# Splitting weights in pieces of 1024 columns from a ring of three, with other rates for the late modulation

## The chip, the cores and the metric

One Trainium2 chip, one core of it. The metric is the device time of one execution in microseconds (us). TensorE runs the matrix products (PE in the profile, its weight loads PEld), VectorE (DVE) and ScalarE (ACT) the elementwise work, GpSimd (POOL) a few small powers, and SyncE (SP) starts nearly all DMA transfers. Each engine works through its own instructions in the order in which they stand; semaphores order the engines among each other.

## The reference

One layer of a diffusion backbone over 256 latent tokens and 256 context tokens, width 2048, in fp32:

```python
h = modulate(rmsnorm(x, norm_mix), sh1, sc1) @ w_in        # and the same for ctx
y_mla = attention(q, k, v)                  # 8 heads, low rank q and kv, latents see all keys
o_dn  = gated_delta_net(q, k, v, g, beta)   # 8 heads, chunks of 64, a scan in each direction
merged = sigmoid(ga) * (y_mla @ w_o_mla) + sigmoid(gb) * (dn_output(o_dn) @ w_o_dn)
x = x + g1 * (merged @ w_out)
gate, val = split(modulate(rmsnorm(x, norm_ffn), sh2, sc2) @ w_ffn_up, 2)
x = x + g2 * ((silu(dwconv(gate)) * val) @ w_ffn_down)
```

The six modulation vectors sh1, sc1, g1, sh2, sc2, g2 are `silu(c) @ w_ada + b_ada`. The hidden width of the feed-forward is 5504.

## The kernel before

Every activation lies transposed in SBUF, features on the 128 partitions and 256 tokens along the free axis. Products with weights are made in two parts: a weight tile `raw` is loaded by DMA, ACT rounds it to `whi` (the fp32r type), and DVE takes `wlo = raw - whi`. Activations are kept in the same way as a pair of 256 columns, high and low. `mm_hl` then makes two matmuls for each 128 rows of depth: `whi` against both parts (512 columns) and `wlo` against the high part (256 columns). On PE these pairs are nearly all of the work.

`load_w` loads a weight row in pieces of up to `GR` = 1024 columns, from a ring of `NR` = 5 places `raw`, and splits each piece in chunks of `GH` = 512 columns from a ring of `NH` = 6 places for `whi` and six for `wlo`. A place comes free for the next load or split when its last reader is done. 1024 columns are eight pairs of matmuls. `lazy_w` calls `load_w` piece by piece as they are needed. The first stage of the kernel (norm, first modulation, first projections, 864 columns each) has its own tiles and does not use the ring.

The stages, in order: the first stage; the heads of the delta net (with their projections, `mmp`); the attention (with products for gates, `gtp`, put in between as filler); the scan of the delta net (with gate products and branch products, `brp`, as filler); the branch products of the delta net; the output projection (`ops`, 16 tiles, each followed by `gather`, which adds the two halves of the product with ACT and DVE into `yx`, then `x1`, its square on ACT, and the sum of squares `ssq` on DVE); the second norm (`ss` a sum over partitions, `ms`, a power on POOL, the broadcast `bc_ps`); the feed-forward (`fps`, 43 tiles each of gate and value); the down projection (`dps`, 16 tiles of depth 43).

`h2_tile(k)` makes one 128-row slice of the normed, modulated input of the feed-forward: `h` on DVE, `h` on ACT, then its high and low parts `H`. The first four feed-forward products (gate and value of tiles 0 and 1) run together over the slices while these are made, in four quarters of 512 columns of the weights.

The late modulation (the vectors g1, sh2, sc2, g2) is work for DVE: 128 tiles `rawa` of 128 x 1024 from `w_ada`, each multiplied with a row of silu(c) (`sch`) and summed in one instruction, followed by one that reads the sum (`parts`). The tiles go through the same ring `raw` and SP's queue as the weights. `ada_rest` is a generator; between its tiles it yields a price, and `Side` runs it as far as the time credited to it allows. `sch` is loaded anew at each change of the half of silu(c), with some yields ahead of the load and behind it. The credits: in the heads `ADB / 22600` of the filler's time, in the attention `AD`, in the scan `ADS` of the step's price, 1500 for each tile of the output projection, 1000 for each of the feed-forward. Three of the four vectors have to be ready before the feed-forward, so what is owed then is run at once:

```python
    while ada.done < 3:
        ada(1)
```

A scheduler places the instructions of each engine; on PE in the first stage and in the heads, the order is the program's.

Of the kernel before, what the change touches and what calls it, by code (L numbers as in the profile page):

```python
# [8 lines left out]
F32 = mybir.dt.float32  # L9
F32R = mybir.dt.float32r  # L10
# [6 lines left out]
P = 128  # L17
D = 2048
KD = D // P
# [6 lines left out]
N1 = 3  # L26
G3 = 96 + 256 * N1
GR = 1024
GH = 512
NR = 5  # L30
NH = 6
AD = 0.55
GD0 = 2
SC = 7500
ON = 3000
# [1 line left out]
CB = 2000  # L37
CC = 7000
RE = 1.0
ADS = 0.3  # L40
OD = 8000
OC = 4000
WO = 1500
# [2 lines left out]
SCP = (2, 5, 7)  # L46
R0 = 1.3
R1 = 1.0
ADB = 4000
SCALE = 192.0 ** -0.5  # L50


# [1 line left out]
def hybrid_block(ctx: ExitStack, tc: tile.TileContext, io, dbg=None):  # L54
    nc = tc.nc
    act, dve, pool, sync = nc.scalar, nc.vector, nc.gpsimd, nc.sync
# [28 lines left out]
    wr = ctx.enter_context(pool_("wr", 2))  # L85
# [31 lines left out]
    def split(raw, hi, lo):  # L117

        act.copy(hi, raw)  # L119
        dve.tensor_tensor(out=lo, in0=raw, in1=hi, op=ALU.subtract)  # L120

    def raw_w(src):
        n = src.shape[1]
        raw = wr.tile([P, GR], F32, tag="raw", name="raw", bufs=NR)[:, :n]
        sync.dma_start(raw, src)
        return raw

    def load_w(src):

        g = []  # L130
        for o in range(0, src.shape[1], GR):
            raw = raw_w(src[:, o : min(o + GR, src.shape[1])])
            for i in range(0, raw.shape[1], GH):
                n = min(GH, raw.shape[1] - i)
                hi = wp.tile([P, GH], F32R, tag="whi", name="whi", bufs=NH)[:, :n]
                lo = wp.tile([P, GH], F32R, tag="wlo", name="wlo", bufs=NH)[:, :n]
                split(raw[:, i : i + n], hi, lo)
                g.append((hi, lo))
        return lambda o, m=P: tuple(w[:, o % GH : o % GH + m] for w in g[o // GH])

    def lazy_w(src):

# [109 lines left out]
    def ada_rest():  # L252


        def load(i):
            w = wr.tile([P, GR], F32, tag="raw", name="rawa", bufs=NR)
            c, n = divmod(i, 32)
            sync.dma_start(w, io["wada2"][c, (n // 16 + c) % 2, n % 16])
            return w

        parts = ad.tile([P, 2, 16], F32, name="parts")
        half, ahead = None, load(0)
        for i in range(128):
            c, n = divmod(i, 32)
            h, j = (n // 16 + c) % 2, n % 16
            if h != half:

                for _ in range(2 if i else 0):
                    yield 1300
                half, sch = h, ad.tile([P, GR], F32, tag="sch", name="sch")  # L270
                sync.dma_start(sch, Sc[h])
                for _ in range(4):
                    yield 1300
            w = ahead
            if i < 127:
                ahead = load(i + 1)
            dve.tensor_tensor_reduce(out=w, in0=w, in1=sch, scale=1.0, scalar=0.0, op0=ALU.mult, op1=ALU.add, accum_out=parts[:, h, j : j + 1])  # L277
            if n == 31:
                cs = slice(16 * c, 16 * c + 16)
                dve.tensor_tensor(out=adaT[:, cs], in0=parts[:, 0], in1=parts[:, 1], op=ALU.add)  # L280
                dve.tensor_tensor(out=adaT[:, cs], in0=adaT[:, cs], in1=bada[:, 32 + 16 * c : 48 + 16 * c], op=ALU.add)
                ada.done = c + 1
            yield 1300
# [1110 lines left out]
    ffn = [(w, f) for f in range(NFF) for w in ("wgate", "wval")]  # L1394
    fps = {j: psm.tile([P, 512], F32, tag="mm", name="fps") for j in ffn[:4]}
    for kq in range(4):
        Ws = [load_w(io[w][f][:, kq * 512 : kq * 512 + 512]) for w, f in ffn[:4]]
        for k in range(4 * kq, 4 * kq + 4):
            h2_tile(k)
            for W, j in zip(Ws, ffn[:4]):  # L1400
                mm_hl(fps[j], P, W(k % 4 * P), H2[:, k], k == 0, k == KD - 1)
    dump("h2", H2.bitcast(F32))
    pM.close()
    pD.close()
# [143 lines left out]
```

## Time and profile before

| | |
|---|---|
| runs | 1860.94 us median of 3 (1857.85 to 1868.06) |
| the profiled execution | 1860.39 us, span 1858.6 us |
| busy time | PE 1788.5, PEld 1527.4, DVE 1376.6, ACT 928.4, POOL 44.3 us |
| `whi` on ACT | 940 instructions, 573.9 us |
| `wlo` on DVE | 940 instructions, 634.0 us |
| `rawa` on DVE | 128 instructions, 156.3 us |
| granted clock of PE | 0.990 in the mean |
| DMA | 419.71 MB, 226 GB/s in the mean |

A row of the grouped view reads: line, engine, operation, output <- inputs, shapes, count | busy time, mean ns of one | idle time of the engine just before, and what ended it. A row of the waits reads: engine, what waited, what it waited for: us in total, times, the longest. A row of the busy times by stretch reads: start and end, width, then busy us (and number) of PE, PEld, DVE, ACT and POOL, the granted clock, the DMA engines' share, GB/s. A row of the timeline reads: start, duration, engine, line, operation, in brackets the idle time before it and what ended it. L68 is the helper that issues pinned instructions and all matmuls, L119 and L120 are the two lines of `split`.

### The profile page before, as it was taken

The page shows a single profiled execution, that of the slowest core. Times are in us where ns is not written, and L with a number is a line of the kernel's source. Part 1 is how long each engine was busy: PE and PEld are TensorE (multiplying, and loading weights), DVE is VectorE, ACT ScalarE, POOL GpSimd, SP SyncE. Part 2 cuts the span into 40 slices and gives each one's busy share as a digit, 9 for nine tenths or more (in the row PEclk, how much of TensorE's full clock was granted, in tenths as well). Part 3 has the DMA queues.
Part 4 walks back from the last instruction along what each step waited for, and adds up shares of the span by engine and source line. Part 5 has one row for each costly group of instructions (what it writes and reads, how often), then busy time and mean ns, then how long its engine had stood idle before and what let it go on. Part 6 is the DMA issues. An engine that isn't in the chain of part 4 may idle for free.

```text
span 1858.6 us, 32954 instructions
## 1 busy us (share of the span) xinstructions
PE 1788.5 (96%) x12386; PEld 1527.4 (82%) x12386; DVE 1376.6 (74%) x2766; ACT 928.4 (50%) x1899; POOL 44.3 (2%) x45
## 2 busy tenths in 40 slices
PE   7899999999999999999999988999999999999999
PEld 4788887888888887778788876888888888888888
DVE  5677889779777876575679888888877788855554
ACT  3335544444666666233346536555555555544443
POOL 0000001000000000000000000000000000000000
PEclk9999999999999999999999998999999999999999
DMA  9992688774677767777757885767766667766663
GB/s 346 342 373 75 178 230 248 202 246 125 207 237 237 224 208 217 260 253 235 244 188 252 293 282 187 251 222 225 224 215 186 211 217 223 263 200 192 196 200 120
DMA packets 195008, 419.71 MB, mean 226 GB/s; under 512 B 61280, under 2 KB 101344, under 8 KB 192416
## 3 DMA queue, kind: packets, MB, share of 16 engines
q1 hardware_dynamic: 167952, 402.39, 67.1%
q10 hardware_dynamic: 26896, 15.21, 2.7%
q8 instruction: 97, 1.59, 0.3%
q14 instruction: 63, 0.52, 0.1%
HBM read 388.57 MB, written 28.84 MB: 225 GB/s over the span
## 4 chain that ended last, share of the span: by engine, by line
PE 54%; DMA 3%; DVE 2%; ACT 1%; issue 1%; POOL 0%; SPq 0%; ACTq 0%; DVEq 0%
PE fps L68 26%; PE dps L68 13%; PE brp L68 5%; PE gtp L68 4%; PE ops L68 3%; DMA rawa<-in_wada 2%; PE op L68 1%; PE kp L68 1%; PE yp L68 1%; DVE wlo L120 1%; DMA raw<-in_wgate 0%; DMA jit<-Vs 0%; DVE rawa L277 0%; DMA yraw<-Ys 0%; DVE S L1284 0%
## 5 line engine op out<-in xcount | busy, mean ns | idle before, releaser
L120 DVE TENSOR_TENSOR wlo<-raw,whi 128x512 fp32r<-128x512 f32 (+1 forms) x940 | 634.0, 686 | 194.5 <-ACT whi L119 185.4
L119 ACT CAST whi<-raw 128x512 fp32r<-128x512 f32 (+1 forms) x940 | 573.9, 619 | 398.4 <-PE dps L68 113.2
L68 PE MATMUL fps<-H,whi 128*128 128x512 f32 x1376 | 481.8, 398 | 5.7 <-DVE H L120 5.7
L68 PE MATMUL fps<-H,wlo 128*128 128x256 f32 x1376 | 374.6, 282 | 0.8 <-DVE wlo L120 0.7
L68 PEld LDWEIGHTS fps<-H,whi 128*128 128x128 f32 x1376 | 253.7, 189 | 62.6 <-issue 5.7
L68 PEld LDWEIGHTS fps<-H,wlo 128*128 128x128 f32 x1376 | 259.2, 188 | 9.4 <-DVE wlo L120 1.9
L68 PE MATMUL gtp<-h,whi 128*128 128x512 f32 x640 | 235.1, 402 | 0.0
L68 PE MATMUL mmp<-h,whi 128*128 128x512 f32 x640 | 228.9, 400 | 0.0
L68 PE MATMUL dps<-GB,whi 128*128 128x512 f32 x560 | 195.9, 391 | 0.0
L277 DVE CUSTOM_DVE_ANT_0 rawa<-rawa,sch 128x1024 f32<-128x1024 f32 x128 | 156.3, 1222 | 49.6 <-DMA rawa<-in_wada 48.6
L68 PE MATMUL gtp<-h,wlo 128*128 128x256 f32 x640 | 175.9, 285 | 1.4 <-DVE wlo L120 1.4
L68 PE MATMUL mmp<-h,wlo 128*128 128x256 f32 x640 | 176.5, 282 | 0.0
L68 PE MATMUL dps<-GB,wlo 128*128 128x256 f32 x560 | 155.3, 282 | 0.0
L68 PEld LDWEIGHTS gtp<-h,whi 128*128 128x128 f32 x640 | 120.7, 189 | 25.5 <-issue 1.2
L68 PEld LDWEIGHTS mmp<-h,whi 128*128 128x128 f32 x640 | 119.1, 188 | 26.2 <-issue 0.4
L68 PEld LDWEIGHTS gtp<-h,wlo 128*128 128x128 f32 x640 | 121.2, 190 | 7.4 <-DVE wlo L120 1.8
L68 PEld LDWEIGHTS dps<-GB,whi 128*128 128x128 f32 x560 | 105.1, 188 | 21.7
L68 PEld LDWEIGHTS mmp<-h,wlo 128*128 128x128 f32 x640 | 120.4, 188 | 2.8 <-issue 0.6
L68 PEld LDWEIGHTS dps<-GB,wlo 128*128 128x128 f32 x560 | 105.9, 189 | 0.6
L68 PE MATMUL fp<-h,gh 128*128 128x256 f32 (+1 forms) x448 | 86.5, 293 | 6.2 <-ACT h L68 5.2
L68 PEld LDWEIGHTS fp<-h,gh 128*128 128x128 f32 (+1 forms) x448 | 70.3, 191 | 12.1 <-ACT h L68 6.4
L496 ACT COPY fx<-fps 128x256 f32<-128x256 f32 x86 | 31.9, 374 | 68.6 <-PE fps L68 68.6
(557 smaller groups left out, 2602.1 us busy)
## 6 DMA issues: line engine op xcount, KB each, us to landing
rawa<-in_wada SPq DMA_DIRECT2D x128, 512.0 KB, 4.6
raw<-in_wgate SPq DMA_DIRECT2D x82, 512.0 KB, 4.3
raw<-in_wval SPq DMA_DIRECT2D x82, 512.0 KB, 4.7
raw<-in_wdown SPq DMA_DIRECT2D x80, 512.0 KB, 4.3
wt<-in_wadas SPq DMA_DIRECT2D x16, 1024.0 KB, 8.0
raw<-in_wadab SPq DMA_DIRECT2D x32, 512.0 KB, 8.1
raw<-in_wgm SPq DMA_DIRECT2D x32, 512.0 KB, 4.8
raw<-in_wgd SPq DMA_DIRECT2D x32, 512.0 KB, 5.2
```

Source lines behind the costliest of these rows:

```text
L68: i = f(*a, **k)
L119: act.copy(hi, raw)
L120: dve.tensor_tensor(out=lo, in0=raw, in1=hi, op=ALU.subtract)
L277: dve.tensor_tensor_reduce(out=w, in0=w, in1=sch, scale=1.0, scalar=0.0, op0=ALU.mult, op1=ALU.add, accum_out=parts[:, h, j : j + 1])
L496: act.copy(out, ps[:M, T:])
```

## The change

Weights are now split in one instruction on each engine for a whole piece of 1024 columns, from a ring of three such places; the columns that the ring holds stay 3072. 940 splits become 480: 460 of 1024 columns, 4 of 512 and 16 of 384 (the last piece of a down-projection tile, which now takes a whole place). For the first four feed-forward products, the quarters of gate and value of one tile are loaded by two transfers into one place and split together. The late modulation is credited more in the heads, the attention and the scan, and has fewer yields at a change of half.

```diff
-GH = 512
-NH = 6
-AD = 0.55
+NH = 3
+AD = 0.6
-ADS = 0.3
+ADS = 0.4
-ADB = 4000
+ADB = 4500
...
+    def raw_w(*srcs):
+        raw, n = wr.tile([P, GR], F32, tag="raw", name="raw", bufs=NR), 0
+        for src in srcs:
+            m = n + src.shape[1]
+            sync.dma_start(raw[:, n:m], src)
+            n = m
+        return raw[:, :n]
+
+    def split_w(raw):
+        n = raw.shape[1]
+        hi = wp.tile([P, GR], F32R, tag="whi", name="whi", bufs=NH)[:, :n]
+        lo = wp.tile([P, GR], F32R, tag="wlo", name="wlo", bufs=NH)[:, :n]
+        split(raw, hi, lo)
+        return hi, lo
 
     def load_w(src):
 
-        g = []
-        for o in range(0, src.shape[1], GR):
-            raw = raw_w(src[:, o : min(o + GR, src.shape[1])])
-            for i in range(0, raw.shape[1], GH):
...
-                split(raw[:, i : i + n], hi, lo)
-                g.append((hi, lo))
-        return lambda o, m=P: tuple(w[:, o % GH : o % GH + m] for w in g[o // GH])
+        g = [split_w(raw_w(src[:, o : min(o + GR, src.shape[1])])) for o in range(0, src.shape[1], GR)]
+        return lambda o, m=P: tuple(w[:, o % GR : o % GR + m] for w in g[o // GR])
...
-                for _ in range(2 if i else 0):
+                for _ in range(1 if i else 0):
                     yield 1300
                 half, sch = h, ad.tile([P, GR], F32, tag="sch", name="sch")
                 sync.dma_start(sch, Sc[h])
-                for _ in range(4):
+                for _ in range(3):
                     yield 1300
...
     for kq in range(4):
-        Ws = [load_w(io[w][f][:, kq * 512 : kq * 512 + 512]) for w, f in ffn[:4]]
+        cs = slice(kq * 512, kq * 512 + 512)
+
+        Ws = [split_w(raw_w(*(io[w][f][:, cs] for w, f in ffn[i : i + 2]))) for i in (0, 2)]
         for k in range(4 * kq, 4 * kq + 4):
             h2_tile(k)
-            for W, j in zip(Ws, ffn[:4]):
-                mm_hl(fps[j], P, W(k % 4 * P), H2[:, k], k == 0, k == KD - 1)
+            for i, j in enumerate(ffn[:4]):
+                o = i % 2 * 512 + k % 4 * P
+                mm_hl(fps[j], P, tuple(w[:, o : o + P] for w in Ws[i // 2]), H2[:, k], k == 0, k == KD - 1)
```

In the changed program the line numbers of the helpers are one lower (`split` is L118 and L119, the helper of pinned instructions L67). The instructions of three places, before and after:

First DVE, from the last tile of the output projection through the second norm to the first slice of the feed-forward's input. `ISA rawa` is a tile of the late modulation, `x_...` the new residual stream. Before:

```order
L497 TENSOR_TENSOR yx<-ops,yx 128x256
L277 ISA rawa,parts<-rawa,sch 128x1024
L277 ISA parts 128x1
L1369 SCALAR_TENSOR_TENSOR x_11698<-yx,adaT,xr 128x256
L277 ISA rawa,parts<-rawa,sch 128x1024
L277 ISA parts 128x1
L1373 TENSOR_TENSOR ssq<-ssq,x1q 128x256
L277 ISA rawa,parts<-rawa,sch 128x1024
L277 ISA parts 128x1
L217 TENSOR_SCALAR ms<-ss 128x2
L280 TENSOR_TENSOR adaT<-parts 128x16
L281 TENSOR_TENSOR adaT<-adaT,vecs 128x16
```

The same place after:

```order
L119 TENSOR_TENSOR wlo<-raw,whi 128x1024
L497 TENSOR_TENSOR yx<-ops,yx 128x256
L1369 SCALAR_TENSOR_TENSOR x_11041<-yx,adaT,xr 128x256
L119 TENSOR_TENSOR wlo<-raw,whi 128x1024
L1373 TENSOR_TENSOR ssq<-ssq,x1q 128x256
L217 TENSOR_SCALAR ms<-ss 128x2
L1389 TENSOR_TENSOR h_11985<-bc_ps,x_11041 128x256
L1389 TENSOR_TENSOR h_11998<-bc_ps,x_11041 128x256
```

The modulation's tiles are gone from this place, and the subtractions for the first two feed-forward weight pieces stand ahead of the norm, where they stood behind it.

Second PE, at the turn from the first to the second quarter of the first four feed-forward products; the number behind `whi` tells the pieces apart. Before:

```order
L68 MATMUL fps_12768<-H2_12765,whi_12784 128x512
L68 MATMUL fps_12768<-H2_12765,wlo_12785 128x256
L68 MATMUL fps_12769<-H2_12765,whi_12790 128x512
L68 MATMUL fps_12769<-H2_12765,wlo_12791 128x256
L68 MATMUL fps_12766<-H2_12765,whi_12848 128x512
L68 MATMUL fps_12766<-H2_12765,wlo_12849 128x256
L68 MATMUL fps_12767<-H2_12765,whi_12854 128x512
L68 MATMUL fps_12767<-H2_12765,wlo_12855 128x256
L68 MATMUL fps_12768<-H2_12765,whi_12860 128x512
L68 MATMUL fps_12768<-H2_12765,wlo_12861 128x256
```

The same place after:

```order
L67 MATMUL fps_11970<-H2_11966,whi_11981 128x512
L67 MATMUL fps_11970<-H2_11966,wlo_11982 128x256
L67 MATMUL fps_11967<-H2_11966,whi_12040 128x512
L67 MATMUL fps_11967<-H2_11966,wlo_12041 128x256
L67 MATMUL fps_11968<-H2_11966,whi_12040 128x512
L67 MATMUL fps_11968<-H2_11966,wlo_12041 128x256
L67 MATMUL fps_11969<-H2_11966,whi_12047 128x512
L67 MATMUL fps_11970<-H2_11966,whi_12047 128x512
L67 MATMUL fps_11967<-H2_11966,whi_12040 128x512
L67 MATMUL fps_11967<-H2_11966,wlo_12041 128x256
L67 MATMUL fps_11968<-H2_11966,whi_12040 128x512
L67 MATMUL fps_11968<-H2_11966,wlo_12041 128x256
```

Two products share a piece now, and the first low parts of the second piece (`wlo_12048`) follow only behind these rows, after the first piece's products with the next slice.

Third ACT, in the middle of the scan; `y` is a step of the scan, `zx` the copy and the tanh of a gate product, `Gs` the DMA that stores it. Before:

```order
L1259 COPY y<-yp 128x512 x2
L119 CAST whi<-raw 128x512 x2
L496 COPY zx<-gtp 128x256
L861 ACTIVATE zx<-zx 128x256
L864 DMA Gs<-zx 128x256
L119 CAST whi<-raw 128x512 x7
L1179 ACTIVATE ox<-brp 128x256
```

The same place after:

```order
L1259 COPY y<-yp 128x512
L118 CAST whi<-raw 128x1024
L496 COPY zx<-gtp 128x256
L861 ACTIVATE zx<-zx 128x256
L864 DMA Gs<-zx 128x256
L118 CAST whi<-raw 128x1024 x3
L1293 COPY o<-op 128x4x64 x4
```

Seven casts of 512 columns behind the gate's copy have become three of 1024.

The 128 tiles of the late modulation stand, by stage, before and after: 17 and 17 in the heads, 37 and 49 in the attention, 17 and 21 in the scan, 27 and 22 from there to the second norm, 30 and 19 behind it.

8 lines of the change are left out of this document (removed).

## The prediction

> **What bounds the kernel now.** I read the page's engine shares first, then the busy time by stage, then the waits of PE (TensorE's matmuls), and last the timeline at the longest of them.
>
> ```profile
> PE 1788.5 (96%) x12386; PEld 1527.4 (82%) x12386; DVE 1376.6 (74%) x2766; ACT 928.4 (50%) x1899; POOL 44.3 (2%) x45
> ```
>
> PE is busy for 1788.5 of the 1858.6 us. The change adds and removes no matmul, so it can win or lose only in the 70 us in which PE stands, and in the clock behind a stall. By stage (first weights, heads, attention, scan, branches and output projection, the pause behind it, first feed-forward tiles, feed-forward):
>
> ```profile
> 0.00:150.00 150.00, 130.35 (x1322) 106.37 (x1323) 98.81 (x145) 55.66 (x119) 2.19 (x8) 0.97 0.88 333
> 150.00:450.00 300.00, 294.05 (x2409) 246.10 (x2408) 250.92 (x540) 138.25 (x290) 20.76 (x19) 1.00 0.65 191
> 450.00:745.00 295.00, 283.55 (x2196) 245.30 (x2195) 217.32 (x464) 190.69 (x428) 17.77 (x16) 0.99 0.71 221
> 745.00:950.00 205.00, 195.10 (x1448) 158.74 (x1448) 132.55 (x321) 67.93 (x142) 0.62 (x1) 0.99 0.76 253
> 950.00:1107.30 157.30, 154.95 (x871) 134.47 (x869) 136.22 (x282) 86.55 (x180) 2.27 (x1) 0.99 0.73 242
> 1107.30:1124.60 17.30, 1.62 (x20) 1.26 (x21) 15.02 (x34) 6.07 (x13) 0.69 (x1) 0.62 0.84 288
> 1124.60:1200.00 75.40, 74.32 (x402) 63.14 (x403) 62.88 (x135) 47.99 (x102) 0.00 (x0) 0.97 0.67 212
> 1200.00:1600.00 400.00, 400.00 (x2269) 347.94 (x2268) 316.51 (x611) 218.40 (x426) 0.00 (x0) 1.00 0.68 218
> ```
>
> The first figure behind the width is PE's busy time. From 1200 to 1600 us it is all of it; 2269 matmuls in 400 us make 0.353 us for a pair (one high, one low part). The first 150 us run before the split's ring exists and stay as they are. PE's other idle time is 6.0 in the heads, 11.5 in the attention, 9.9 in the scan, 2.4 up to 1107.3, and 15.7 in one pause of 17.3 us. Who ends it:
>
> ```profile
> PE ss L68 <- DVE ssq L1373: 8.6, 1, 8.6
> PE fps L68 <- DVE H L120: 5.7, 2, 5.5
> ...
> PE brp L68 <- ACT whi L119: 4.4, 2, 2.4
> ...
> PE gtp L68 <- DVE wlo L120: 1.4, 2, 0.9
> ```
>
> Two waits, both in the pause, are the largest; the two that a split weight ends and that are over 1 us come to 5.8 us in four stalls.
>
> **The pause, and what the change leaves of it.** The late modulation's tiles that are still owed are run in one block before the second norm; here is what stands in PE's way.
>
> ```profile
> 1106.90 0.40 PE L68 MATMUL ops<-MB,whi 128*128 128x512 f32 x1
> ...
> 1115.46 0.42 DVE L1373 TENSOR_TENSOR ssq<-ssq,x1q 128x256 f32<-128x256 f32 x1
> ...
> 1115.80 1.22 DVE L277 CUSTOM_DVE_ANT_0 rawa<-rawa,sch 128x1024 f32<-128x1024 f32 x1
> 1115.93 0.40 PE L68 MATMUL ss<-ones,ssq 128*32 128x1 f32 x16 [8.64 <-DVE ssq L1373]
> ...
> 1116.94 0.16 DVE L217 TENSOR_SCALAR ms<-ss 128x2 f32<-128x2 f32 x1
> ...
> 1117.92 1.22 PE L68 MATMUL bc_ps<-ident,ms 128*128 128x128 f32 x4 [1.59 <-POOL ms L171]
> ...
> 1121.47 0.75 DVE L1389 TENSOR_TENSOR h<-bc_ps,x 128x256 f32<-128x256 f32 x2
> ...
> 1122.62 1.09 ACT L1390 ACTIVATE h<-h,adaT,a 128x256 f32<-128x256 f32 x2
> ...
> 1123.62 0.69 ACT L119 CAST H<-h 128x256 fp32r<-128x256 f32 x2
> 1124.04 0.76 DVE L120 TENSOR_TENSOR H<-h,H 128x256 fp32r<-128x256 f32 x2 [0.59 <-ACT H L119]
> ...
> 1124.61 0.76 PE L68 MATMUL fps<-H,whi 128*128 128x512 f32 x1 [5.46 <-DVE H L120]
> ```
>
> The last product ends at 1107.30, the next real one starts at 1124.61. In the changed program no modulation tile stands between the last gather and the norm (the part on the change), and the first two split weight pieces stand ahead of it. How fast that chain is undisturbed shows at the kernel's end, where nothing else runs:
>
> ```profile
> 1854.11 0.40 PE L68 MATMUL dps<-GB,whi 128*128 128x512 f32 x1
> 1854.55 0.37 ACT L496 COPY yo<-dps 128x256 f32<-128x256 f32 x1 [7.59 <-PE dps L68]
> 1854.95 0.42 DVE L497 TENSOR_TENSOR yo<-dps,yo 128x256 f32<-128x256 f32 x1 [7.40 <-ACT yo L496]
> 1855.41 0.48 DVE L1443 SCALAR_TENSOR_TENSOR yo<-yo,adaT,x 128x256 f32<-128x256 f32 x1
> ```
>
> PE's end to the end of x: 1.38 us. Then one weight piece stands on DVE (1.22, below), while ACT squares; then ssq 0.42: 3.05 where it is 8.63 now. Sum to broadcast: ms starts at 1116.94, behind a modulation tile, though the sum ends at 1116.33; 0.61 falls away. The broadcast's 1.22 stays. From its end (1119.14) to PE's start it is 5.47 now; with DVE and ACT free it is h 0.42, the two activations 1.09, the cast 0.40 and the subtraction 0.42 with 0.15 between them, 2.5: 2.95 falls away. Together 5.6 + 0.6 + 2.95 = 9.1 us; the pause shrinks to about 8.2. Bounds: 12 won if ssq is not behind the weight piece (1.2) and the slow clock goes too (1.8, next), 5 won if both weight pieces and the feed-forward weights' landing get in the way again.
>
> The clock behind a stall:
>
> ```profile
> 1124.83:1128.24 3.41, 3.41 (x11) 2.93 (x12) 2.66 (x7) 2.10 (x6) 0.00 (x0) 0.50 0.48 133
> ...
> 950.75:954.16 3.41, 1.21 (x7) 0.73 (x5) 1.82 (x6) 1.04 (x2) 1.52 (x1) 1.00 0.00 0
> 954.16:957.57 3.41, 3.41 (x13) 2.83 (x12) 2.85 (x10) 1.48 (x4) 0.00 (x0) 0.53 0.60 163
> 957.57:960.98 3.41, 3.41 (x20) 2.99 (x20) 2.67 (x8) 1.57 (x4) 0.00 (x0) 0.96 0.07 29
> ```
>
> These are stretches of 3.41 us. One in which PE worked 1.21 is followed by one at half clock (0.53), with 13 matmuls where the next has 20; behind the pause there are 11 at 0.50, which loses 9/20 of 3.41, and the 0.2 us ahead of it a little: 1.8 us with all. So a pause of 8.2 us, with short matmuls inside it, still ends in a slow stretch; I take no gain. The Trainium skill (TensorE: Matmul & The Clock Gate, What's actually happening) says that the clock halves after at least one idle window of about 3.4 us; none of the new pause's idle pieces (3.05, 1.4, 2.5 us) fills a window, so by that rule the sum would be 1.8 us lower. The rows above show the half clock behind a stretch with 2.2 us of idle time, and the trace decides.
>
> **Wider splits.** Four forms on the same engines give the price:
>
> ```profile
> L120 DVE TENSOR_TENSOR wlo<-raw,whi 128x512 fp32r<-128x512 f32 x924 | 625.1, 689 | 185.1 <-ACT whi L119 176.0 <-DMA Ud<-U 0.7 <-DMA Gs<-zx 0.7
> L68 DVE TENSOR_TENSOR gl<-gr,gh 128x864 fp32r<-128x864 f32 x16 | 16.9, 1057 | 16.5 <-ACT gh L68 16.5
> L119 ACT CAST whi<-raw 128x512 fp32r<-128x512 f32 x924 | 565.7, 620 | 386.1 <-PE dps L68 100.9 <-PE fps L68 93.1 <-PE mmp L68 54.2
> L68 ACT CAST gh<-gr 128x864 fp32r<-128x864 f32 x16 | 14.6, 914 | 1.8 <-PE fp L68 1.0 <-ACT h L68 0.8
> ```
>
> DVE: 368 ns for 352 more columns, so 1024 cost 1057 + 167 = 1.22 us against 2 x 0.689; ACT: 294 ns for 352, so 1.05 against 2 x 0.620. Of 940 splits 460 pairs merge: 460 x 0.154 = 71 us less on DVE, 460 x 0.19 = 87 us less on ACT. PE hides nearly all of it: from 1200 to 1600 it has no idle time to give. Where PE does wait for DVE and ACT (27 us from 150 to 950), about 5% less work there would be 1.4 us; I take -1.0, bounds -3 and 0. The Trainium skill (VectorE: DVE Perf Modes, The TRN2 errata) puts the fixed cost at about 150 cycles an instruction and advises larger tiles; by that rule, were DVE the bound, 460 x 151 / 0.96 GHz = 72 us would go. The trace's 71 us agrees, but not that they are on the path.
>
> Against it stands the latency. A piece was 4 pairs, 1.4 us of PE, six deep: when a place came free, five pieces (7.0 us) were ahead and the refill took 0.62 + 0.69 = 1.3, a slack of 5.7. Now a piece is 2.8 us, three deep: 5.6 ahead, refill 1.05 + 1.22 = 2.3, slack 3.3. In the feed-forward DVE has at most 1.25 us (a gather and two steps of the convolution) between two weight pieces, or 2.5 with a modulation tile: it fits, cost 0. The weight waits that there are lie in the scan, and come from the order on ACT:
>
> ```profile
> 843.70 0.37 ACT L496 COPY zx<-gtp 128x256 f32<-128x256 f32 x1 [4.13 <-PE gtp L68]
> ...
> 845.38 3.22 ACT L119 CAST whi<-raw 128x512 fp32r<-128x512 f32 x6 [0.40 <-ACT zx L861]
> ...
> 846.05 0.50 PE L68 MATMUL brp<-YM,whi 128*128 128x512 f32 x1 [2.38 <-ACT whi L119]
> ```
>
> ACT stood 4.13 us for the end of a gate product, its casts queued behind the copy and the tanh of the result; PE then waited 2.38 us for the first of them. The changed order has the same turn with three wide casts behind it. Each such first cast is 0.43 longer, at two such stalls: I take +1.0; bounds -5.8 (all weight waits vanish) and +3 (these four and two new ones, half a us more each).
>
> **First feed-forward tiles.** As many bytes in as many transfers, but two to a place: eight splits for sixteen. At the turn from one quarter to the next the second piece needs the place that PE leaves two pairs (0.7 us) before the turn; its low part is there 2.3 us later, 1.6 behind the turn. The old row of matmuls asked for it 0.9 behind the turn; the new one puts six others first (1.9). Cost 0; bounds -1.1 (all idle time of this stage today) and +2.1 (three turns at 0.7).
>
> **The modulation's rates.** By the program's order 49 of the 128 tiles fall into the attention where 37 did, 21 into the scan for 17, 22 between scan and feed-forward for 27, with no block among them, and 19 into the feed-forward for 30. The feed-forward wins nothing (no idle time). The attention has 11.5 us of idle PE at 37 tiles; if that grew with the tiles, 12 more would cost 3.7, and hidden they cost 0. Each is 1.2 us of DVE and a 512 KB load in the shared queue, and a weight split behind it waits as long. I take +1.5.
>
> **Sum.** The profiled execution took 1860.4 us (0.5 below the median of 1860.94): -9.1 -1.0 +1.0 +0 +1.5 = -7.6, so 1852.8, or 1853.3 against the median. I say 1853, a gain of 0.4%. A change of 0.5% (9.3 us) is about what a measurement of this kernel can tell from none.
>
> **Rivals.**
> The queues gain: the pause closes and the shorter ACT and DVE work also thins the idle time of heads, attention and scan (27 us) by a sixth, 4.5 us, in place of the +1.5 and -1.0: 1848. For it: the 87 us on ACT, and waits for whi. Against: each item at the head of a queue is longer. (No slow stretch behind the pause alone gives 1851, inside the forecast.)
> The ring of three is too short: wherever more than 3.3 us of DVE work, a modulation tile's late landing included, comes ahead of a piece, PE stands. From half a us in each of 43 feed-forward steps on it decides: 21 us lost, 9 won, 1872. Against: 400 us without an idle PE today, and no two modulation tiles in a row there.
> The pause closes but all comes back: scan and attention lose 8 us (a third more idle time and two more slow stretches): 1861.
>
> **Chances.** Forecast 0.46 (1851.6 to 1859.3), gaining queues 0.36, all back 0.08, ring too short 0.10. Faster by over 0.5%: 0.36. Within: 0.46 + 0.08 = 0.54. Slower: 0.10. The range, 1845 to 1865, takes in the first two cases and half of the third and leaves about 0.15 outside; the forecast's own is 1851 to 1859.
>
> **What would show it.** PE's wait for ssq near 3 us and for H near 2.5 in place of 8.6 and 5.5; no run of rawa tiles ahead of ms; wlo at 1.22 and whi at 1.05 us; PE without idle time through the feed-forward; PE's waits for whi and wlo near 8 us. I am wrong if these last reach 20, if the attention's idle time passes 16 us, or if the pause stays over 11.

## The result, and the profile after

| | before | after |
|---|---|---|
| runs, median | 1857.99 us (14 runs, 1853.57 to 1868.86) | 1875.23 us (14 runs, 1866.62 to 1882.65) |
| profiled execution | 1860.39 us | 1866.62 us |
| mean granted clock of the runs | 0.988 (25 later runs) | 0.987 (14 runs) |

After is slower: ratio 1.0086, 95% interval 1.0068 to 1.0103, some 16 us by the ratio and 17 between the medians. Medians and ratios here and below are of the runs in the common, fast state, so one run each of two later kernels, of 2183 and 7993 us, is left out. The profiled execution of after is the shortest of its 14 and shows only 6.2 us of the loss; where in the kernel the rest lies, no trace of after shows. The clock explains little of the 16: a mean clock of 0.987 over 1873 us is some 49 us at half clock, and at the prediction's 9/20 of a us for each that loses 22 us; before, the same sum gives 20.4. The other 14 us aren't the granted clock.

The page's engine shares of after:

```profile
PE 1794.1 (96%) x12386; PEld 1528.0 (82%) x12386; DVE 1330.6 (71%) x2306; ACT 855.5 (46%) x1439; POOL 45.1 (2%) x45
```

DVE is busy 46 us less than before, ACT 73 us, and the kernel is longer. Busy time of after by stage (heads, attention, scan, branches, output projection, pause, feed-forward), cut here where each stage's last product ends:

```profile
150.10:444.96 294.86, 288.97 (x2368) 240.76 (x2367) 242.33 (x476) 125.75 (x229) 18.63 (x17) 1.00 0.66 191
444.96:731.06 286.10, 274.92 (x2132) 236.11 (x2131) 220.95 (x429) 178.28 (x360) 17.85 (x15) 0.99 0.76 235
731.06:942.97 211.91, 199.98 (x1352) 164.37 (x1351) 131.82 (x279) 65.67 (x103) 2.74 (x3) 0.97 0.76 253
942.97:1022.70 79.73, 76.74 (x545) 65.44 (x545) 69.89 (x140) 43.74 (x79) 3.00 (x1) 1.00 0.69 222
1022.70:1121.36 98.66, 93.11 (x513) 78.83 (x511) 77.75 (x123) 43.99 (x65) 0.00 (x0) 0.98 0.85 284
1121.36:1128.92 7.56, 1.02 (x21) 0.77 (x21) 3.95 (x9) 3.42 (x7) 0.70 (x1) 0.83 0.61 196
1128.92:1621.17 492.25, 488.98 (x2753) 424.10 (x2754) 369.31 (x583) 244.08 (x369) 0.00 (x0) 1.00 0.66 204
```

The pause went from 17.3 to 7.6 us. The output projection, which had no idle PE before, went from 89.7 to 98.7: in this execution, what the pause gave is lost in the stage ahead of it. Lengths by the same cut in eleven profiles, those of the experiments below among them (one execution each; us):

| kernel | median | first | heads | attention | scan | branches | output proj. | pause | feed-forward |
|---|---|---|---|---|---|---|---|---|---|
| before | 1858.0 | 151.8 | 293.7 | 282.0 | 209.2 | 80.9 | 89.7 | 17.3 | 490.3 |
| after | 1875.2 | 150.1 | 294.9 | 286.1 | 211.9 | 79.7 | 98.7 | 7.6 | 492.2 |
| rates alone | 1869.8 | 150.2 | 293.2 | 291.7 | 214.2 | 80.8 | 90.7 | 9.7 | 493.6 |
| splits alone | 1872.3 | 148.0 | 293.3 | 281.5 | 216.7 | 79.8 | 94.5 | 13.5 | 491.8 |
| two instructions a piece | 1859.8 | 151.8 | 299.0 | 277.8 | 211.6 | 81.5 | 91.7 | 7.0 | 491.3 |
| before, no loads | 1828.3 | 150.2 | 290.2 | 275.0 | 195.8 | 80.8 | 89.8 | 10.4 | 488.4 |
| after, no loads | 1830.1 | 151.8 | 294.2 | 272.3 | 196.3 | 79.8 | 89.7 | 8.2 | 491.2 |
| rates alone, no loads | 1831.3 | 153.0 | 290.8 | 275.1 | 196.1 | 80.8 | 89.8 | 7.4 | 491.7 |
| only the subtraction in two | 1864.6 | 151.4 | 295.1 | 276.8 | 216.6 | 81.2 | 95.7 | 7.5 | 491.8 |
| modulation's own places | 1855.6 | 153.6 | 295.9 | 302.2 | 194.1 | 80.8 | 89.9 | 7.5 | 494.4 |
| own place for every second tile, new rates | 1866.1 | 150.0 | 290.5 | 294.7 | 205.1 | 81.4 | 97.3 | 7.5 | 493.5 |

The down projection takes 239.6 to 240.0 us in all eleven. The first stage, which no version changes, takes 148.0 to 153.6, so a difference of a few us in one stage of two single executions can't be told from none. PE's waits after:

```profile
PE ops L67 <- DVE wlo L119: 5.5, 6, 2.5
PE ks L67 <- ACT ksq L978: 4.3, 2, 3.4
PE kp L67 <- DVE r L1248: 3.9, 5, 1.7
PE brp L67 <- DMA raw<-in_wgd: 2.9, 1, 2.9
```

The first is new: the output projection waits for low parts. The longest of these waits, on DVE (start, duration, in brackets the idle time ahead and who ended it):

```profile
1094.28 1.23 DVE L119 TENSOR_TENSOR wlo<-raw,whi 128x1024 fp32r<-128x1024 f32 x1
1098.09 1.23 DVE L277 CUSTOM_DVE_ANT_0 rawa<-rawa,sch 128x1024 f32<-128x1024 f32 x1 [2.58 <-DMA rawa<-in_wada]
...
1099.23 0.42 DVE L497 TENSOR_TENSOR yx<-ops,yx 128x256 f32<-128x256 f32 x1
1099.57 1.22 DVE L277 CUSTOM_DVE_ANT_0 rawa<-rawa,sch 128x1024 f32<-128x1024 f32 x1
...
1100.71 0.48 DVE L1369 SCALAR_TENSOR_TENSOR x<-yx,adaT,xr 128x256 f32<-128x256 f32 x1
1101.11 1.22 DVE L119 TENSOR_TENSOR wlo<-raw,whi 128x1024 fp32r<-128x1024 f32 x1
```

and the same moment on PE and ACT:

```profile
1099.45 0.40 PE L67 MATMUL ops<-MA,whi 128*128 128x512 f32 x1
1102.38 0.56 PE L67 MATMUL ops<-MA,wlo 128*128 128x256 f32 x1 [2.54 <-DVE wlo L119]
```

```profile
1094.98 1.05 ACT L118 CAST whi<-raw 128x1024 fp32r<-128x1024 f32 x1 [0.46 <-DMA raw<-in_wout]
```

The high part is ready at 1096.03. DVE stands until 1098.09 for a modulation tile that hasn't landed, then has that tile, a gather, a second tile and the residual ahead of the subtraction, which starts at 1101.11, five us after its input. PE reaches the piece at 1099.45 and stands 2.54 us for a result that DVE had time for while it stood itself. SP had issued the loads of the two tiles late, from 1091.97 on, when DVE had already begun the tile before them (at 1090.71):

```profile
1091.97 2.32 SPq L258 DMA_DIRECT2D rawa<-in_wada  x2
```

Over the kernel DVE stands at the head of its queue for these tiles (us, times, longest), before and then after:

```profile
DVE rawa L277 <- DMA rawa<-in_wada: 48.6, 41, 4.0
```

```profile
DVE rawa L277 <- DMA rawa<-in_wada: 63.2, 48, 3.6
```

### The profile page after: what moved, and what is told of

Its sections match the earlier page's. It is cut to its first block, busy times and chain, and to the rows that moved or that the text cites. A ratio compares the mean times of both kernels' runs of the same rounds, so it can differ in the third digit from the quotient of the medians.

```text
span 1864.8 us, 31779 instructions
## 1 busy us (share of the span) xinstructions
PE 1794.1 (96%) x12386; PEld 1528.0 (82%) x12386; DVE 1330.6 (71%) x2306; ACT 855.5 (46%) x1439; POOL 45.1 (2%) x45
## 4 chain that ended last, share of the span: by engine, by line
PE 44%; issue 10%; DMA 3%; DVE 3%; ACT 1%; POOL 0%; SPq 0%; ACTq 0%; POOLq 0%; DVEq 0%
PE fps L67 22%; PE dps L67 13%; PE gtp L67 4%; DMA rawa<-in_wada 2%; PE brp L67 2%; DVE wlo L119 1%; PE op L67 1%; PE kp L67 1%; PE yp L67 1%; ACT whi L118 0%; DMA raw<-in_wgd 0%; DVE rawa L277 0%; DVE S L1284 0%; DMA Gs<-zx 0%; DMA yraw<-Ys 0%
## 5 line engine op out<-in xcount | busy, mean ns | idle before, releaser
L119 DVE TENSOR_TENSOR wlo<-raw,whi 128x1024 fp32r<-128x1024 f32 (+1 forms) x480 | 572.9, 1196 | 211.6 <-ACT whi L118 209.5
L118 ACT CAST whi<-raw 128x1024 fp32r<-128x1024 f32 (+1 forms) x480 | 492.4, 1028 | 316.5 <-PE dps L67 136.9
L67 PE MATMUL fps<-H,whi 128*128 128x512 f32 x1376 | 481.6, 398 | 4.4 <-DVE H L119 4.4
L67 PE MATMUL fps<-H,wlo 128*128 128x256 f32 x1376 | 374.0, 282 | 1.4 <-DVE wlo L119 1.4
L67 PEld LDWEIGHTS fps<-H,whi 128*128 128x128 f32 x1376 | 253.7, 189 | 60.5 <-issue 2.6
L67 PEld LDWEIGHTS fps<-H,wlo 128*128 128x128 f32 x1376 | 259.1, 188 | 10.2 <-DVE wlo L119 2.3
L67 PE MATMUL gtp<-h,whi 128*128 128x512 f32 x640 | 233.6, 400 | 0.0
L67 PE MATMUL mmp<-h,whi 128*128 128x512 f32 x640 | 229.2, 400 | 0.0
L277 DVE CUSTOM_DVE_ANT_0 rawa<-rawa,sch 128x1024 f32<-128x1024 f32 x128 | 156.2, 1222 | 65.6 <-DMA rawa<-in_wada 63.2
L67 PE MATMUL dps<-GB,whi 128*128 128x512 f32 x560 | 195.9, 391 | 0.0
L67 PE MATMUL gtp<-h,wlo 128*128 128x256 f32 x640 | 175.7, 284 | 1.6 <-DVE wlo L119 1.6
L67 PE MATMUL mmp<-h,wlo 128*128 128x256 f32 x640 | 176.2, 281 | 0.0
L67 PE MATMUL dps<-GB,wlo 128*128 128x256 f32 x560 | 155.2, 282 | 0.0
L67 PEld LDWEIGHTS mmp<-h,whi 128*128 128x128 f32 x640 | 119.0, 188 | 26.1 <-ACT dkx L508 0.3
L67 PEld LDWEIGHTS gtp<-h,whi 128*128 128x128 f32 x640 | 120.1, 189 | 24.5 <-issue 0.8
L67 PEld LDWEIGHTS gtp<-h,wlo 128*128 128x128 f32 x640 | 120.7, 189 | 8.5 <-DVE wlo L119 3.5
L67 PEld LDWEIGHTS dps<-GB,whi 128*128 128x128 f32 x560 | 105.1, 188 | 21.8
L67 PEld LDWEIGHTS mmp<-h,wlo 128*128 128x128 f32 x640 | 120.3, 188 | 2.8 <-issue 0.6
L67 PEld LDWEIGHTS dps<-GB,wlo 128*128 128x128 f32 x560 | 105.8, 189 | 0.6
L67 PE MATMUL fp<-h,gh 128*128 128x256 f32 (+1 forms) x448 | 84.9, 289 | 7.6 <-ACT h L67 6.7
L67 PEld LDWEIGHTS fp<-h,gh 128*128 128x128 f32 (+1 forms) x448 | 68.9, 188 | 13.5 <-ACT h L67 7.8
```

What stands on the lines that cost most here:

```text
L67: i = f(*a, **k)
```

## Experiments: each part alone

The first theory was the ring of three; its rival the rates. Rates alone is the kernel before with these lines:

```diff
-AD = 0.55
+AD = 0.6
-ADS = 0.3
+ADS = 0.4
-ADB = 4000
+ADB = 4500
...
-                for _ in range(2 if i else 0):
+                for _ in range(1 if i else 0):
...
-                for _ in range(4):
+                for _ in range(3):
```

Splits alone is after with the same lines undone. The third is after with chunks and ring of 512 put back (`GH = 512`, `NH = 6`), new rates and paired loads kept.

> The kernel before with only the modulation's new rates (and fewer yields); splits of 512 columns from a ring of six stay. Ring theory (the loss comes from places of 1024 columns that come free late, so that a low part queued on VectorE behind a late modulation tile reaches PE late): the pause before the second norm shrinks from 17.3 to about 8 us, the output projection keeps its 90 us without a PE wait, and the time falls to about 1850 (1846 to 1853). Rates theory (more modulation tiles in attention and scan, as in the profile of after: 4.1 and 2.7 us longer): the pause shrinks too, but 7 us come back there, so 1856 to 1860.

Measured: 1869.78 us, ratio 1.0069 [1.0045, 1.0093].

> The changed kernel with the old rates and yields: splits of 1024 columns from a ring of three, and the first feed-forward weights in pairs. Ring theory: the pause stays near 17 us, and PE still waits some 5 us for wlo in the output projection, where as many modulation tiles land late as before: 1866 to 1876. Rates theory: the splits alone are harmless, 1855 to 1859.

Measured: 1872.25 us, 1.0077 [1.0048, 1.0106].

> The changed kernel, its weights split in 512 columns again from a ring of six places of 512; the new rates and the paired loads of the first feed-forward weights stay. Ring theory: about 1850, as with the rates alone (the paired loads cost nothing within 2 us). Rates theory: 1856 to 1860. If the paired loads are the loss: above 1860, and longer than the rates alone by 5 us or more between the norm and the 200 us behind it.

Measured: 1869.44 us, 1.0052 [1.0030, 1.0075].

Neither theory holds alone. The rates lose 11.6 us without any wide split, more than the rates theory had; the splits (with their ring of three and the paired loads) lose 14.1 without the rates; both together lose about as much as either. The pause and the output projection together are 6.6 us shorter with the rates alone (table), and attention and scan 14.7 longer. The paired loads show nothing: 0.3 us between the medians with and without them. Losses that don't add point to a cause that both share; that it is shared is so far only argued.

## Experiments: which property of the wide split

After with the cast and the subtraction of a piece in two instructions each, the place and the ring of three kept:

```diff
-        split(raw, hi, lo)
+        for o in range(0, n, 512):
+            e = min(o + 512, n)
+            split(raw[:, o:e], hi[:, o:e], lo[:, o:e])
```

> The changed kernel with its places of 1024 columns and ring of three, but each piece cast and subtracted in two instructions of 512 columns, so that the first half is ready 0.43 + 0.53 us earlier and VectorE and ScalarE work as long as before. If the place's late release is the cause (PE frees 1024 columns at once): 1868 to 1876, with the waits for wlo in the output projection as in after. If the longer instructions are (one piece's 2.3 us from free place to low part): the time falls back to about 1850 to 1856.

Measured: 1859.76 us, 1.0011 [0.9993, 1.0029], some 4 us above the second range but as long as the kernel before. The late release of the place isn't the cause, since it is as late here; the long instruction is, whether by its own length or because PE gets the whole piece at once. The next two cut one engine's instruction only, first the subtraction, then the cast:

```diff
-        split(raw, hi, lo)
+        act.copy(hi, raw)
+        for o in range(0, n, 512):
+            e = min(o + 512, n)
+            dve.tensor_tensor(out=lo[:, o:e], in0=raw[:, o:e], in1=hi[:, o:e], op=ALU.subtract)
```

> The changed kernel with only the subtraction in two instructions of 512 columns (1.38 us in all on VectorE, the first half ready 0.5 us earlier); the cast stays one of 1024. The two halves together gave back 14 us (1875 to 1860). Theory VectorE (a low part, or what stands behind it, is late by the long subtraction): 1860 to 1864. Theory ScalarE (the long cast stands ahead of the scan's and the attention's own copies, and of the subtraction): 1870 to 1876.

Measured: 1864.6 us, 1.0034 [1.0013, 1.0055].

```diff
-        split(raw, hi, lo)
+        for o in range(0, n, 512):
+            e = min(o + 512, n)
+            act.copy(hi[:, o:e], raw[:, o:e])
+        dve.tensor_tensor(out=lo, in0=raw, in1=hi, op=ALU.subtract)
```

> The changed kernel with only the cast in two instructions of 512 columns; the subtraction stays one of 1024 columns, 1.22 us, and starts as late as in after or later. Theory VectorE: 1870 to 1876. Theory ScalarE: 1860 to 1864. If each engine's part counts for half: 1866 to 1869 for both kernels.

Measured: 1877.73 us, 1.0091 [1.0063, 1.0118]. The long subtraction on VectorE carries it: cutting it gave back 10.6 us, cutting the cast alone none. (Cutting the cast as well gave 4.8 us more, by the ratios 1.0034 and 1.0011 too little to tell from none.) The profile of the kernel with only the cast cut has more of the same wait:

```profile
PE ops L67 <- DVE wlo L136: 8.8, 8, 1.8
PE gtp L67 <- DVE wlo L136: 5.0, 6, 2.6
```

the one with only the subtraction cut has somewhat less than the 5.5 us of after:

```profile
PE ops L67 <- DVE wlo L136: 3.9, 4, 1.8
```

and the one with both cut has least:

```profile
PE ops L67 <- DVE wlo L119: 1.7, 1, 1.7
```

So the output projection is not all of it: with the subtraction alone cut it is still 95.7 us long, and that profile wins most in the attention (286.1 to 276.8) and loses in the scan (211.9 to 216.6). Two short subtractions cost DVE 0.16 us more than a long one (2 x 0.69 against 1.22), but PE need not wait for the second: in the one stall left with both cut, PE goes on at 1107.71 us with the first half, and DVE starts on the second at 1107.90. The rates once more, on this form (two instructions a piece, old rates):

> Places of 1024 columns in a ring of three, split in two instructions of 512 on each engine (as in the kernel that came out at 1860), with the old rates and yields: the pause is back to about 17 us. If the rates lose as much here as with the ring of six (12 us): 1848 to 1850. If they lose nothing, since what they win at the pause (9 us) covers the rest: 1858 to 1863. If they win: 1866 and above.

Measured: 1868.27 us, 1.0040 [1.0021, 1.0058]. Here the new rates win 8.5 us between the medians, or 5 by the ratios (1.0040 against 1.0011), which is just clear of their intervals; with the ring of six they lost 11.6. So the rates have no fixed price; what they cost depends on the rest of the kernel. What in it decides was not settled.

## Experiments: without the loads

These kernels leave out the loads of the 128 modulation tiles (67 MB of 420); DVE multiplies as often and as long (1.22 us), on a tile in SBUF. The vectors that come out have other values, which the program first uses in the residual behind the output projection; up to there PE multiplies the same numbers as before.

```diff
-            sync.dma_start(w, io["wada2"][c, (n // 16 + c) % 2, n % 16])
...
-            dve.tensor_tensor_reduce(out=w, in0=w, in1=sch, ...)
+            dve.tensor_tensor_reduce(out=w, in0=sch, in1=sch, ...)
```

> The changed kernel without the loads of the late modulation's 128 tiles (64 MB less to move); VectorE makes the same multiplications, in the same place, on a tile that lies in SBUF. Theory late landing (VectorE stands 63 us for these tiles, and the subtractions queue behind them): the waits for wlo in the output projection fall from 5.5 to under 1.5, that stage to some 91 us, the whole to 1855 or below. Theory instruction length alone (no DMA in it): 1868 to 1875, the output projection 95 us or longer.

Measured: 1830.1 us, 0.9844 [0.9819, 0.9870]: 45 us less than after. The output projection of this kernel, with as much work on DVE (78.0 us, in after 77.8):

```profile
994.30:1084.02 89.72, 89.72 (x513) 78.19 (x511) 78.00 (x120) 44.54 (x65) 0.00 (x0) 1.00 0.70 216
```

PE has no idle time in it, at 216 GB/s where after has 284. The kernel before had none either, at 278 GB/s:

```profile
1017.00:1107.30 90.30, 90.30 (x516) 78.71 (x514) 74.27 (x138) 45.91 (x91) 0.00 (x0) 1.00 0.82 278
```

So among these three the late tiles alone don't stop PE there, and neither do the long subtractions; the two together do. Attention and scan are 13.8 and 15.6 us shorter than in after. Then the same on the kernel before and on the rates alone:

> The kernel before without the loads of the late modulation's 128 tiles; VectorE makes the same multiplications on a tile that lies in SBUF. Late landing (the tiles' loads cost through VectorE's queue): clearly shorter than before, but by less than the changed kernel gained (45 us), since the places of 512 columns ride out more of it: 1825 to 1840, with the block of modulation tiles ahead of the second norm still 14 us of VectorE and the pause near 17. If the landing hurts only where a subtraction is 1024 columns long: 1852 to 1860.

Measured: 1828.31 us, 0.9832 [0.9805, 0.9860].

> The new rates with splits of 512 columns in a ring of six, without the loads of the late modulation's tiles. Late landing: without it the rates show what the prediction priced, the pause of 17 us falls to 8 and nothing comes back in attention and scan: 9 us (7 to 12) shorter than the kernel before without these loads, and within 3 us of the changed kernel without them (1830), since the width of a split then lies beside PE's work. If the rates themselves cost in attention and scan (VectorE's time, not the landing): as long as the kernel before without the loads, or longer.

Measured: 1831.31 us, 0.9850 [0.9826, 0.9875].

This is the main finding. With the loads, the change costs 17 us between the medians; without them the three kernels are within 3.0 us: wide or narrow splits, ring of three or six, old or new rates all take 1828 to 1831 (each interval is some 5 us either way). What the change costs, it costs only where these loads are made. The expected 9 us for the rates did not show. The time is that of the theory that the rates cost in attention and scan, but the stages deny it: these two are as long as in the kernel before without the loads (table). The pause of that kernel is only 10.4 us, so there were just 3.0 to win, and the first stage and the feed-forward are 2.8 and 3.3 us longer: part of the 17.3 was the loads too.

The loads do three things at once: a tile that lands late holds up DVE's queue; its place in the ring of five is held while it loads; and it takes DMA time. Leaving the loads out does not take the tiles out of the ring: the products are still written to their places, and the weights' loads wait for them, for longer than the 37.0 us of after:

```profile
SPq L125 <- DVE parts L276: 210.4, 63, 11.5
```

So sharing five places with the tiles is not by itself what costs the weights their time. DVE's waits for tiles in after, in the attention and then in the output projection:

```profile
DVE rawa L277 <- DMA rawa<-in_wada: 17.2, 14, 2.5
```

```profile
DVE rawa L277 <- DMA rawa<-in_wada: 19.2, 13, 2.6
```

In the scan it stood for none, and that stage still gained 15.6 us, so there it must be one of the other two. A trace points at the place: in after's scan SP, which works in order, stood six times and 24.9 us in all for a place for the next tile, with the loads behind it standing too, and PE waited 2.9 us for a weight that had not landed (`raw<-in_wgd` above). That the place costs more than the transfer is not shown by these runs.

## Experiments: having the tiles earlier

Loads issued two tiles ahead, on after and on the form with two instructions a piece:

```diff
-        half, ahead = None, load(0)
+        half, ahead = None, [load(0), load(1)]
...
-            w = ahead
-            if i < 127:
-                ahead = load(i + 1)
+            w = ahead.pop(0)
+            if i < 126:
+                ahead.append(load(i + 2))
```

> The changed kernel with each modulation tile's load issued one tile earlier (two tiles ahead of its use, from the same ring of five places). Late landing: VectorE's idle time before these tiles falls from 63 us to under 35, and the time to 1855 to 1866. Rival: the second tile takes a place from the weights in the ring, the weights land later, and the time stays at 1870 to 1885.

Measured: 1871.64 us, 1.0067 [1.0044, 1.0090]. DVE's idle time before the tiles fell from 63.2 to this:

```profile
DVE rawa L277 <- DMA rawa<-in_wada: 54.9, 47, 3.6
```

The time is in the rival's range. A load that stands one tile earlier in the program left SP hardly earlier: from its issue to its product the median tile had 6.3 us where after had 5.9.

> Places of 1024 columns split in two instructions of 512, the new rates, and the modulation's loads two tiles ahead. Late landing: 1845 to 1855, shorter than both kernels. Rival (the weights lose a place in the ring): 1860 to 1872.

Measured: 1856.47 us, 0.9996 [0.9976, 1.0017]: the same as the kernel before, and in neither range.

Then two places of their own for the modulation's tiles, paid with two places of the split's ring, and the control with only the smaller ring:

```diff
-NH = 6
+NH = 4
...
-            w = wr.tile([P, GR], F32, tag="raw", name="rawa", bufs=NR)
+            w = wp.tile([P, GR], F32, tag="rawa", name="rawa", bufs=2)
```

> The kernel before (old rates, splits of 512) with two places of their own for the modulation's tiles beside the five places for weights; the split's ring pays for them, four places of 512 instead of six. With a place of their own the tiles run earlier: all 128 stand before the second norm, 47 of them by the end of the heads. Theory shared ring (a tile lands late since its load waits for a place that a subtraction frees): VectorE's idle time before these tiles falls from 49 to under 20 us, the block before the norm is gone, and the time is 1835 to 1850. Theory transfer time (the DMA engines' share, not the place, makes them late): idle time stays above 40 us and the time at 1856 or above.

Measured: 1855.56 us, 0.9985 [0.9972, 0.9998].

> The kernel before with only the split's ring cut from six places of 512 columns to four (2048 columns), the control for the kernel with the modulation's own places. If depth of the ring is what keeps late tiles off PE: 1863 to 1880, with waits for wlo in the output projection as in the changed kernel. If depth doesn't matter here: 1855 to 1862.

Measured: 1872.11 us, 1.0089 [1.0062, 1.0115].

The depth of the split's ring does matter by itself, 14 us for two of six places, but not where I expected it: the output projection stays at 90.2 us, the attention grows from 282.0 to 286.6 and the feed-forward from 490.3 to 497.6. In the feed-forward PE's waits for low parts go from 0.7 us to this:

```profile
PE fps L68 <- DVE wlo L120: 2.5, 7, 0.8
```

At this depth the own places win 16.5 us (1872.1 to 1855.6). DVE's idle time before the tiles:

```profile
DVE rawa L277 <- DMA rawa<-in_wada: 31.0, 31, 2.9
```

That is between the two theories' numbers (under 20, above 40), so the shared places are a part of the lateness, not all; the time is within a us of the second theory's. All 128 tiles now stand before the second norm, 61 of them in the attention, which grows to 302.2 us (in a profiled execution 8 us above the median); the scan, with 6 of them, takes 194.1, as it does without the loads, though every load is still made somewhere. The last three ask for the same at other prices. First with a ring of two places of 1024 (`NH = 2`), two instructions a piece:

> Places of 1024 columns split in two instructions of 512, a ring of two such places, the new rates, and two places of their own for the modulation's tiles. Theory shared ring: 1835 to 1852, if two places of 1024 columns (5.6 us of PE) are enough for the weights. Theory transfer time, or a split ring that is too short: 1858 and above.

Measured: 1879.97 us, 1.0125 [1.0099, 1.0150], in the second range, which stands for two theories. PE waits for low parts at three kinds of product (6.3 us at `kps`, 5.2 at `gtp`, 4.0 at `mmp`), which speaks for too short a ring.

Then one own place, for every second tile, paid with one place of 512, loads two ahead, with the new rates and the old:

```diff
-NH = 6
+NH = 5
...
-            w = wr.tile([P, GR], F32, tag="raw", name="rawa", bufs=NR)
+            w = wp.tile([P, GR], F32, tag="rawa", name="rawa", bufs=1) if i % 2 else wr.tile([P, GR], F32, tag="raw", name="rawa", bufs=NR)
```

> The new rates, splits of 512 from a ring of five places (one given up), and for every second modulation tile a place of its own, the others in the shared ring, loaded two ahead. Theory shared ring: VectorE's idle time before the tiles falls from 48 us (rates alone) to under 40 and the time from 1870 to 1845 to 1857, the pause at 8 us. Rival (depth of the split's ring: six to four places cost 14 us): 1862 to 1872.

Measured: 1866.13 us, 1.0050 [1.0035, 1.0065]. DVE's idle time before the tiles did not fall from 48 us to under 40 but rose to 77.8.

> The same places with the old rates: the block of modulation tiles ahead of the second norm is back. Theory shared ring: 1848 to 1858. Rival (ring of five too short): 1860 to 1870. If the rates themselves cost (12 us as with a ring of six), it is shorter than its twin with the new rates; if the pause counts, longer by 5 to 9 us.

Measured: 1866.51 us, 1.0048 [1.0028, 1.0067]; DVE stood 50.6 us for tiles. Both times are the rival's numbers, but they don't show the ring of five as the cause, since the own place brought the tiles no earlier. The twins are equal: here the rates neither cost nor win. In both the output projection is long again, 97.3 and 95.8 us, and PE stands there 4.2 and 4.7 us for low parts, though all subtractions are short. A long subtraction is one way to lose time behind a late tile, not the only one. No version is faster than the kernel before by more than 0.15% (two own places, 1855.6 us, with an interval that just leaves out 1). This one and the one with two instructions a piece and two loads ahead (1856.5) are 1% faster than the changed kernel.

## Why the prediction was wrong

It said 1853 with a range of 1845 to 1865, and gave slower by over 0.5% a chance of 0.10; it came out 0.86% slower. What failed is the step that put the latency of the wide pieces at cost 0, and beside it the term for the rates, since neither gave the loads of the late tiles a price. By its steps:

**The pause: right in the profile.** Forecast 8.2 us, measured 7.6; won 9.7 of 17.3, forecast 9.1. Most of the difference is the broadcast, kept at 1.22 us and measured at 0.71. The rows that it named:

```profile
1124.36 0.30 PE L67 MATMUL ss<-ones,ssq 128*32 128x1 f32 x16 [3.00 <-DVE ssq L1373]
...
1125.73 0.71 PE L67 MATMUL bc_ps<-ident,ms 128*128 128x128 f32 x4 [1.06 <-POOL ms L171]
...
1128.92 0.77 PE L67 MATMUL fps<-H,whi 128*128 128x512 f32 x1 [2.49 <-DVE H L119]
```

Expected 3.05 and 2.5. The clock behind it, by stretches of 3.41 us:

```profile
1119.50:1122.91 3.41, 1.86 (x12) 1.37 (x10) 2.30 (x4) 1.53 (x4) 0.00 (x0) 1.00 0.96 332
1122.91:1126.33 3.42, 0.91 (x20) 0.74 (x20) 1.56 (x3) 0.29 (x1) 0.70 (x1) 1.00 0.63 178
1126.33:1129.74 3.41, 0.92 (x4) 0.75 (x4) 2.14 (x6) 1.89 (x5) 0.00 (x0) 0.50 0.25 97
1129.74:1133.16 3.42, 3.42 (x12) 2.94 (x12) 1.47 (x5) 2.50 (x7) 0.00 (x0) 0.50 0.00 0
```

The half clock came back, as the prediction took it. No stretch was wholly idle: PE worked 0.91 us in the second, and half clock follows. The rule that the prediction quoted from the Trainium skill (TensorE: Matmul & The Clock Gate, What's actually happening), an idle window of about 3.4 us before the clock halves, would have left it at full speed; the trace disagrees, with 0.50 behind a stretch in which PE was busy for a quarter.

**Wider splits: the durations were right, the worth wrong.** The groups of after:

```profile
L119 DVE TENSOR_TENSOR wlo<-raw,whi 128x1024 fp32r<-128x1024 f32 x460 | 561.2, 1222 | 193.9 <-ACT whi L118 191.8
L118 ACT CAST whi<-raw 128x1024 fp32r<-128x1024 f32 x460 | 481.8, 1049 | 287.7 <-PE dps L67 109.3 <-PE fps L67 86.4 <-PE mmp L67 28.0
```

1.22 and 1.05 us, to the digit. (The 71 and 87 us saved are right as sums of durations; the page's busy time, in which overlapping records count once, fell by 46 and 73.) But the term was -1.0, and the splits alone, with the ring of three, measured +14.1.

**The latency of the wide pieces in a ring of three: this step failed.** It put the slack at 3.3 us where it had been 5.7, weighed it against at most 2.5 us of DVE work between two pieces, looked only at the feed-forward, and wrote cost 0. In the feed-forward that was right (from 1200 to 1600 us PE stands 0.4 us). The output projection was not weighed: it had no idle PE before. It grew by 9.0 us, with 5.5 us of waits for low parts. There DVE's standing for a late tile (2.6 us), two tiles, a gather and a residual come between the cast and the subtraction, five us in the rows above. The rival "ring too short" had the right mechanism, "a modulation tile's late landing included", but the wrong place: it was priced over 43 feed-forward steps and then discounted by the 400 us without idle time. And its name was off: with the same ring of three but short instructions the loss is gone (1859.8 us). That accounts for the output projection; how the loads cost in the attention and the scan stays open.

**The modulation's rates: mis-sized.** +1.5 (bounds 0 to +3.7) for attention and scan; the rates alone lose 11.6 net of what they win at the pause: 9.7 longer in attention and 5.0 in the scan. The prediction scaled idle PE time with the number of tiles. The loads were counted as "a 512 KB load in the shared queue" and given no price; without them the new rates lengthen attention and scan by 0.4 us in all.

**The weight waits in the scan and the first feed-forward tiles.** The +1.0 for first casts behind a gate's copy did not show in after: PE's waits for `whi` at the branch products fell from 4.4 to 1.8 us. (With the splits alone they were 6.6, so this term moves with the order of the rest.) PE's waits for `whi` and `wlo` together were forecast near 8 us; they came to 11.6 in after (9.8 of it for `wlo`), below the 20 that I had named as the sign of being wrong. Nor did the two other signs show: PE's idle time in the attention is 11.2 us, the pause 7.6. The profiled execution is 9 us under the median of the runs, and signs read from one execution were too coarse for this loss. Paired loads: 0, as forecast.

**PE's work was not constant.** The prediction let the change act only in PE's 70 idle us and in the clock behind a stall. PE's busy time went from 1788.5 to 1794.1 us, with about as long at half clock in both profiles (38 and 39 us), so the clock explains little of these 5.6 us, and they stay open.

## What to carry to other kernels

Of an engine that works in order, ask first what stands at its head waiting for a DMA and how long the work queued behind it is, not how busy it is: DVE was idle over a quarter of the time here, and longer instructions on it made the kernel slower. A stage in which PE never stands may have just enough buffers for its late loads; before making instructions longer or rings coarser, look at the stages with a high DMA rate (here 284 GB/s in the output projection, against 204 in the feed-forward). Leaving out a background load shows in one run what its being there costs, here 30 to 45 us, though not in which way.

## What the runs showed of the hardware

Leaving out 67 MB of 420 MB shortened this kernel and its variants by 30 to 45 us though PE was busy 96% of the time: its own busy time fell as well, in after from 1794.1 to the 1780.5 us of this row without the loads.

```profile
PE 1780.5 (97%) x12386; PEld 1524.2 (83%) x12386; DVE 1336.6 (73%) x2306; ACT 855.0 (47%) x1439; POOL 46.8 (3%) x45
```

The same 12386 matmuls run 13.6 us shorter, with 24 us at half clock instead of 39 (the stretches of the two profiles added up), which by the prediction's 9/20 is 7 us of it: a stall that brings the half clock is paid twice, once as idle time and once more in the stretch behind. The other half of the 13.6 us is not explained.
